# Fewer slots for two experts, norms by scaled transposes, and a modulation group weighed by VectorE

## The chip, the cores and the metric

The kernel runs on one core of one Trainium2 chip. The core has a matrix engine (TensorE, PE in the rows), three engines for element-wise work (VectorE or DVE, ScalarE or ACT, GpSimd or POOL) and SyncE (SP), whose instructions here do little but start transfers. Sixteen DMA engines move data between memory and the core. The metric is the device time of one execution in microseconds; before the change it is 1521.48 us, the median of three runs.

## What is computed

The reference is a two-layer network over 256 latent tokens and 256 context tokens of width 1024. Each layer has a token mixer (attention, retention and pooling between one input and one output projection) and then a channel mixer, each between two norms. The channel mixer of the first layer is a dense gated block for both streams. That of the second layer sends each of the 256 latent tokens to two of eight experts. Cut to what the change touches:

```python
for i in range(2):
    sh1, sc1, g1, sh2, sc2, g2 = split(silu(c) @ w_mod[i] + b_mod[i], 6)   # and the same from c_ctx
    hx = rms_norm(x, norm_pre_mix[i]) * (1 + sc1) + sh1
    x = x + g1 * rms_norm(token_mixers(hx, hc, ...), norm_post_mix[i])
    hx = rms_norm(x, norm_pre_ffn[i]) * (1 + sc2) + sh2
    x = x + g2 * rms_norm(ffn(hx), norm_post_ffn[i])     # dense in layer 0, experts in layer 1

def swiglu(h, w1, w3, w2):                                # 1024 -> 2816 -> 1024
    return (silu(h @ w1) * (h @ w3)) @ w2

def moe_swiglu(h, router, w1, w3, w2):
    top_vals, top_idx = lax.top_k(h @ router, 2)          # two experts for each token
    gates = sum(one_hot(top_idx, 8) * softmax(top_vals)[..., None], axis=-2)
    return sum(gates[..., e:e+1] * swiglu(h, w1[e], w3[e], w2[e]) for e in range(8))
```

Everything is float32. With the reference's inputs the router gives the eight experts 15, 154, 50, 25, 52, 46, 80 and 90 tokens.

## The kernel before

One program runs through five stages: setup, the first layer's mixer, the dense block, the second layer's mixer, and the experts. The order of each engine's instructions is set when the program is built, by a scheduler that starts from the order of the text and what each instruction needs; a block of text can be held back behind another instruction (`behind`). Buffers come from pools by a tag; a new tile of a tag with all its buffers in use waits for the readers of the oldest one.

**Experts.** Each expert has a fixed number of slots (`SLOTS`), and only that many rows are computed for it. Position 0 is expert 0; positions 1 to 7 are the other experts by falling number of tokens, which VectorE works out from the router's result. `RUNS` says in which order the positions are computed: position 0 first, then 2, 4, a run with two positions side by side, 5, 3, 7. The two that share a run are position 1, which has 160 slots in two parts of 128 and 32, and position 6 with 64. If any expert has more tokens than slots, a loop behind the output goes through its weights again for the rest.

The weights of one expert are 33 blocks of 1 MB: 22 of w1 and w3 in turn (`up`), and 11 of w2 (`down`). SyncE loads them in that order (`wload`, L172) into a ring of 13 buffers; six more are lent once at the start of the stage. A load waits until the ring's next buffer has been read. For a part of 128 slots each matrix product is done in three passes (`mm3`, L235 to L237) on operands that VectorE and ScalarE split into a high and a low half (L161, L162). For fewer slots it is plain float32 with the features as the stationary operand, and several matmuls stand side by side in the array: with 64 slots two of 64 rows by 256 columns, with 32 slots four of 32 rows by 128 columns (L1339 in `up`; L1368 in `down`, with 512 and 256 columns). A matmul of the text in float32 shows as two records in the trace.

The rows of an expert's tokens come to the core in two ways. For position 0 matmuls with a selection matrix `P` pick them (L1281). For the others the kernel writes all rows scaled by their norm to a table in memory (`xrows`), works out the numbers of the rows (`index`, L1223), gathers them with an indirect DMA (`fetch`, tile `xr`), and transposes them (L1278, in `gather`). This is done for the next run while the matmuls of `up` of the current one go on. In `act` the products become activations: silu on ScalarE, a product on VectorE, transposes on TensorE (L1306), tiles `mg`. `scatter` writes the results to memory; the last run instead adds its own to the sum of the others (`add_up`, `adder`, `combine`).

**Norms.** `prenorm` makes the transposed and modulated features of a block of 256 tokens. It is called four times: for the context (m = 1) and the latents (m = 0) ahead of the dense block, and for both ahead of the second layer's mixer. The rows are in two tiles of 128x1024. VectorE works out the reciprocal norm of each row (L444, L150 to L157) and multiplies a 128x128 identity with it (`diag`, L544); sixteen matmuls with the rows stationary and the diagonal moving scale and transpose in one (L551). Then come scale and shift (L559 on VectorE, and the same on ScalarE) and the split into halves.

**Modulation.** The vectors `sh1` to `g2` are products of silu(c) with `w_mod`, in groups of eight blocks of 1 MB (`mod_group`). The first `split` blocks of a group are weighed on VectorE (L369 for the first, L367 for the others, two instructions of 128x1024 a block and stream) and their sums are folded on TensorE at the end; the other blocks are multiplied on TensorE (L373). The last groups are pulled in as filler, a block at a time, between the steps of the dense block and of the second mixer (`fill`); the one that the change touches is group 2 of layer 1, for the latents alone, with `split` = `SPL` = 4.

Of the kernel before, what the change touches and what calls it, by code (L numbers as in the profile page):

```python
# [10 lines left out]
F32 = mybir.dt.float32  # L11
# [3 lines left out]
OP = mybir.AluOpType  # L15
# [5 lines left out]
D = 1024  # L21
KB = 8
# [7 lines left out]

SLOTS = (64, 160, 128, 128, 64, 64, 64, 64)

RUNS = ((0,), (2,), (4,), (1, 6), (5,), (3,), (7,))
SCRATCH = 4096
RING2, RING3 = 3, 6
MA = 3
NFILL, SPL, FILLS = 2, 4, (1, 1)
SPIN0, SPIN1, SPIN2 = 15, 5, 2  # L40

C_ID, C_TRI, C_IOTA, C_I8, C_CAP, C_TOK, C_ROW, C_COS, C_SIN, C_END = \
# [3 lines left out]
def shape_constants():  # L46
# [5 lines left out]
    c[:, C_I8:C_I8 + 8] = np.arange(8)  # L52
    c[:, C_CAP:C_CAP + 8] = SLOTS
    p = np.arange(128)
# [42 lines left out]
class Net:  # L97
# [437 lines left out]
    def prenorm(self, l, which, m, hh, hl):  # L535


        nc = self.nc
        A, B = self.modc[l][which], self.modc[l][which + 1]
        x = self.res_t[2 * m:2 * m + 2]  # L540
        diag = self.s2([128, 2, 128], "diag")
        for n in range(2):
            r = self.rstd([[x[n]]], [self.junk()])
            nc.vector.tensor_scalar(diag[:, n], self.ident, r[:, 0:1], None, op0=OP.mult)  # L544
        c = slice(256 * m, 256 * m + 256)
        for k0 in range(0, KB, 2):
            p = self.mm() if k0 % 4 and (l == 0 or m) else self.at()
            for k in range(2):
                for n in range(2):
                    s = 256 * k + 128 * n  # L550
                    nc.tensor.matmul(p[:, s:s + 128], lhsT=x[n][:, (k0 + k) * 128:(k0 + k + 1) * 128], rhs=diag[:, n],  # L551
                                     start=True, stop=True)
            h = self.s2([128, 2, 256], "h")
            for k in range(2):
                a, b = A[:, m, k0 + k:k0 + k + 1], B[:, m, k0 + k:k0 + k + 1]
                if k0 % 4:
                    nc.scalar.activation(h[:, k], p[:, 256 * k:256 * k + 256], AF.Identity, scale=a, bias=b)
                else:
                    nc.vector.tensor_scalar(h[:, k], p[:, 256 * k:256 * k + 256], a, b, op0=OP.mult, op1=OP.add)  # L559
            self.split(hh[:, k0:k0 + 2, c], hl[:, k0:k0 + 2, c], h)  # L560
# [596 lines left out]
    def experts(self, pool):  # L1157
        nc, I = self.nc, self.I
# [29 lines left out]
        p = self.at()  # L1188
        for t in range(2):
            for s in range(t + 1):  # L1190
                nc.tensor.matmul(p[:, t * 8:t * 8 + 8], lhsT=tri if s == t else onesr, rhs=sel[:, s],
                                 start=s == 0, stop=s == t)
# [64 lines left out]
            return xr, few  # L1257

        def group(n):
            return pool.tile([128, 4, 8 * n], F32, name="few", tag=f"few{n}", bufs=1 + n // 64)  # L1260

        def gather(base, n, rk=None, w=None, got=None):

            xr, few = got or (None, None)
            if xr is None:
                P = places("P", base, n, rk, w, 1)
            if n < 128:
                few = few or group(n)
                xs = few[:, 0].rearrange("p (k s) -> p k s", s=n)
# [3 lines left out]
            for q in range(2):  # L1273
                p = self.at()
                for k in range(4):
# [4 lines left out]
                    for t in range(2):  # L1280
                        nc.tensor.matmul(p[:, k * 128:k * 128 + n], lhsT=res[t][:, d:d + 128], rhs=P[:, t, :n],  # L1281
                                         start=t == 0, stop=t == 1)
                xg = xs[:, 4 * q:4 * q + 4] if n < 128 else pool.tile([128, 4, 128], F32, name="xg", tag="xg", bufs=1)
                for k in range(4):
                    kk = 4 * q + k
                    a, b = A[:, 0, kk:kk + 1], B[:, 0, kk:kk + 1]
# [4 lines left out]
                s = slice(4 * q, 4 * q + 4)  # L1291
# [132 lines left out]
        def ready(pos, t):  # L1424


            ns = [min(128, SLOTS[pos] - b) for b in range(0, SLOTS[pos], 128)]
            t[pos] = ns, [], []
# [45 lines left out]
        def last_sums():  # L1474
            pos, = RUNS[-1]
            return adder(0, SLOTS[pos], lambda t: rankp[:, t, pos:pos + 1], lambda t: gatep[:, t, pos:pos + 1], True)

# [79 lines left out]
        for i, run in enumerate(RUNS):  # L1557
# [5 lines left out]
            for pos in run:  # L1563
                ns, xs, _ = cur[pos]
# [11 lines left out]
            for c, aTs in enumerate(zip(*ups)):  # L1576
# [3 lines left out]
                else:  # L1580
                    hold.close()
                    if i == 0:
                        cur[0][2].append(index(0, 0, SLOTS[0])[1:])
            finish(side)
# [175 lines left out]
```

## Time and profile before

| | us |
|---|---|
| median of three runs (lowest, highest) | 1521.48 (1519.68, 1522.76) |
| the profiled execution: device time | 1520.14 |
| the profiled execution: span of the trace | 1517.9 |

| engine | busy us | share of the span | instructions |
|---|---|---|---|
| PE, matmuls | 1452.5 | 96% | 9006 |
| PEld, weight loads of TensorE | 1053.9 | 69% | 9007 |
| DVE | 823.6 | 54% | 1551 |
| ACT | 616.4 | 41% | 983 |
| POOL | 62.5 | 4% | 93 |

The trace covers one execution; its span starts with the first and ends with the last instruction, 2.2 us less than the device time. The table's shares are means over the five stages. The seven runs of the experts take from 800 us to 1502 us of the span, and the dense block ends with its norms between 635 and 660 us. The mean granted clock of TensorE is 0.985 of full speed. 410.8 MB are moved in all.

### The profile page before, as it was taken

Reading aid. Unit: us, or ns where it says so; the run is one execution under the profiler, and the core shown is the slowest. Engines: PE = TensorE matmul, PEld = TensorE weight load, DVE = VectorE, ACT = ScalarE, POOL = GpSimd, SP = SyncE. Lnnn points to the kernel's source line nnn. Section 1 sums busy time; section 2 is a strip of 40 time slices with the busy share of each in tenths; the row PEclk is TensorE's granted clock in tenths of the full one; section 3 lists DMA queues with packets and bytes.
Section 4 is the critical chain, followed back from the end, with each engine's and each line's share of the span. In section 5 each row is a group of like instructions: output and inputs, shape, how many; then the busy total and the mean of one; then the engine's idle time right before and its main releaser. Section 6 shows DMA issues by size and latency. Waiting matters only on the chain.

```text
span 1517.9 us, 22725 instructions
## 1 busy us (share of the span) xinstructions
PE 1452.5 (96%) x9006; PEld 1053.9 (69%) x9007; DVE 823.6 (54%) x1551; ACT 616.4 (41%) x983; POOL 62.5 (4%) x93
## 2 busy tenths in 40 slices
PE   7999999999999999999998999999999998999996
PEld 5677667988878888788665477764666655477762
DVE  3496687774554545778763088622454341078612
ACT  4336654423222222456641177522343331177511
POOL 1010200000000001000000010000000001010000
PEclk9999999999999999999999999999999999999998
DMA  8773223344453525353379899999998899999994
GB/s 340 278 285 146 86 98 123 141 170 163 142 206 135 207 100 186 119 186 111 118 293 420 351 416 368 370 403 419 419 355 329 326 363 393 420 421 409 409 420 180
DMA packets 62995, 410.82 MB, mean 271 GB/s; under 512 B 9428, under 2 KB 10136, under 8 KB 15648
## 3 DMA queue, kind: packets, MB, share of 16 engines
q1 hardware_dynamic: 54864, 392.19, 66.1%
q0 software_dynamic: 5616, 16.29, 2.9%
q8 instruction: 73, 1.20, 0.3%
q10 hardware_dynamic: 2400, 0.79, 0.2%
q14 instruction: 42, 0.34, 0.1%
HBM read 402.27 MB, written 6.98 MB: 270 GB/s over the span
## 4 chain that ended last, share of the span: by engine, by line
PE 84%; DVE 6%; DMA 5%; ACT 3%; issue 2%; ACTq 0%; POOL 0%; DVEq 0%; POOLq 0%
PE mm L1339 12%; PE mm L236 11%; PE mm L235 11%; PE mm L237 11%; PE mm L1368 7%; PE at L235 7%; PE at L236 7%; PE at L237 6%; PE md L373 1%; PE at L747 1%; DVE whl L162 1%; DMA more<-yrows 1%; DMA xr<-xrows,src 1%; PE at L724 1%; DMA few<-xrows,src 1%
## 5 line engine op out<-in xcount | busy, mean ns | idle before, releaser
L162 DVE TENSOR_TENSOR whl<-w,whl 128x1024 fp32r<-128x1024 f32 x310 | 374.5, 1223 | 267.6 <-ACT whl L161 259.2
L161 ACT ACTIVATE whl<-w 128x1024 fp32r<-128x1024 f32 x310 | 323.7, 1058 | 294.0 <-PE at L237 174.1
L1339 PE MATMUL mm<-w,few 128*64 128x256 f32 (+2 forms) x2528 | 225.8, 347 | 0.0
L1339 PEld LDWEIGHTS mm<-w,few 128*64 128x64 f32 (+1 forms) x2528 | 147.6, 133 | 68.6 <-issue 17.7
L1368 PE MATMUL mm<-w,few 128*64 128x512 f32 (+1 forms) x616 | 111.2, 536 | 0.0
L235 PE MATMUL mm<-hh,whl 128*128 128x512 f32 (+1 forms) x256 | 95.7, 374 | 1.2 <-ACT hh L161 1.2
L236 PE MATMUL mm<-hl,whl 128*128 128x512 f32 (+1 forms) x256 | 95.9, 375 | 0.0
L237 PE MATMUL mm<-hh,whl 128*128 128x512 f32 (+1 forms) x256 | 95.5, 373 | 0.0
L1368 PEld LDWEIGHTS mm<-w,few 128*64 128x64 f32 (+1 forms) x616 | 35.0, 129 | 70.6 <-issue 68.3
L237 PE MATMUL mm<-whl,hl 128*128 128x256 f32 (+1 forms) x240 | 80.9, 342 | 0.0
L236 PE MATMUL mm<-whl,hh 128*128 128x256 f32 (+1 forms) x224 | 75.3, 338 | 1.8 <-DVE whl L162 1.8
L1303 DVE TENSOR_TENSOR mg<-mg,mm 128x256 f32<-128x256 f32 (+2 forms) x36 | 13.6, 378 | 114.2 <-ACT mg L1302 114.2
L235 PE MATMUL mm<-whl,hh 128*128 128x256 f32 (+1 forms) x224 | 74.8, 338 | 0.0
L236 PE MATMUL at<-hl,whl 128*128 128x512 f32 (+1 forms) x192 | 71.3, 371 | 0.0
L237 PE MATMUL at<-hh,whl 128*128 128x512 f32 (+1 forms) x192 | 71.3, 371 | 0.0
L235 PE MATMUL at<-hh,whl 128*128 128x512 f32 (+1 forms) x192 | 71.2, 371 | 0.0
L367 DVE SCALAR_TENSOR_TENSOR wsum<-w,sc,wsum 128x1024 f32<-128x1024 f32 x48 | 59.7, 1281 | 20.8 <-DMA w<-in_w_mod_dram 20.8
L1302 ACT ACTIVATE mg<-mm 128x256 f32<-128x256 f32 (+3 forms) x54 | 22.8, 422 | 117.7 <-PE mm L1339 113.1
L235 PE MATMUL mm<-whl,xh 128*128 128x512 f32 (+1 forms) x144 | 57.9, 402 | 7.5 <-ACT whl L161 7.5
L236 PE MATMUL mm<-whl,xh 128*128 128x512 f32 (+1 forms) x144 | 57.2, 397 | 2.8 <-DVE whl L162 2.8
L235 PEld LDWEIGHTS mm<-hh,whl 128*128 128x128 f32 x256 | 48.2, 188 | 11.3 <-issue 2.1
L237 PE MATMUL mm<-whl,xl 128*128 128x512 f32 (+1 forms) x144 | 55.6, 386 | 0.0
(492 smaller groups left out, 2604.1 us busy)
## 6 DMA issues: line engine op xcount, KB each, us to landing
w<-in_moe_w_dram SPq DMA_DIRECT2D x258, 1024.0 KB, 11.5
w<-in_w_mod_dram SPq DMA_DIRECT2D x48, 1024.0 KB, 6.0
w<-in_ffn_w_dram SPq DMA_DIRECT2D x33, 1024.0 KB, 4.9
w<-in_w_in_dram SPq DMA_DIRECT2D x16, 1024.0 KB, 4.9
w<-in_w_out_dram SPq DMA_DIRECT2D x8, 1024.0 KB, 5.5
wa<-in_moe_w_dram SPq DMA_DIRECT2D x3, 1024.0 KB, 9.7
gate<-gscr POOLq DMA_DIRECT2D x5, 512.0 KB, 4.8
band<-in_band_dram SPq DMA_DIRECT2D x4, 512.0 KB, 7.8
```

The lines of the kernel that those rows point to most:

```text
L161: self.nc.scalar.activation(hi, x, AF.Copy)
L162: self.nc.vector.tensor_sub(lo, x, hi.bitcast(F32))
L235: mm(out, lhsT=a[0], rhs=b[0], start=start, stop=False)
L236: mm(out, lhsT=a[0], rhs=b[1], start=False, stop=False)
L237: mm(out, lhsT=a[1], rhs=b[0], start=False, stop=stop)
L367: nc.vector.scalar_tensor_tensor(x, y, c, x, op0=OP.mult, op1=OP.add)
L373: nc.tensor.matmul(p[32 * j:32 * j + 32], lhsT=self.sc[:, k], rhs=w[:, 0, j * 512:(j + 1) * 512], start=k == split, stop=k == KB - 1 and n ...
L724: nc.tensor.matmul(sp[:, :n], lhsT=qT[:, h, t * 128:t * 128 + 128], rhs=kT[:, kv, j, c0:], start=j == 0, stop=j == 1)
L747: nc.tensor.matmul(op[64 * i:64 * i + 64, side * 256:side * 256 + 256], lhsT=vt[:, b + 2 * side, kv * 64:kv * 64 + 64], rhs=src[:, b], sta ...
L1302: nc.scalar.activation(s1[:r, :c], h1[:r, :c], AF.Silu)
L1339: nc.tensor.matmul(h[i][m * j:m * j + m, :c], lhsT=x[0][:, k], rhs=t[:, k - k0, j * c:j * c + c], start=k == 0, stop=k == KB - 1, tile_pos ...
L1368: nc.tensor.matmul(y[0][m * q:m * q + m, :c], lhsT=x[0][:, b], rhs=w[:, j, c * q:c * q + c], start=f + j == 0, stop=f + j == FB - 1, tile_ ...
```

## The change

Four things change.

1. Position 0 and position 7, the one with the fewest tokens, get 32 slots instead of 64. Position 7 takes the place beside position 1, and position 6 goes into the last run.
2. `prenorm` no longer makes a diagonal. VectorE scales the rows themselves into a new tile `xs` (four instructions of 128x512 a call), and TensorE transposes them against the identity, in the same sixteen steps.
3. `SPL` goes from 4 to 8 (`KB`): all eight blocks of the last modulation group are weighed by VectorE.
4. The `few` tiles of 32 slots get two buffers like those of 64, and the tile `xg` of `gather` moves from a tag of its own with one buffer to the tag `mg`, which has two.

```diff
-SLOTS = (64, 160, 128, 128, 64, 64, 64, 64)
+SLOTS = (32, 160, 128, 128, 64, 64, 64, 32)
-RUNS = ((0,), (2,), (4,), (1, 6), (5,), (3,), (7,))
+RUNS = ((0,), (2,), (4,), (1, 7), (5,), (3,), (6,))
-NFILL, SPL, FILLS = 2, 4, (1, 1)
+NFILL, SPL, FILLS = 2, KB, (1, 1)
...
     def prenorm(self, l, which, m, hh, hl):
         x = self.res_t[2 * m:2 * m + 2]
-        diag = self.s2([128, 2, 128], "diag")
-        for n in range(2):
-            r = self.rstd([[x[n]]], [self.junk()])
-            nc.vector.tensor_scalar(diag[:, n], self.ident, r[:, 0:1], None, op0=OP.mult)
+        r = [self.rstd([[x[n]]], [self.junk()]) for n in range(2)]
+        xs = [self.s4([128, D], "xs") for _ in range(2)]
+        for half in range(2):
+            for n in range(2):
+                c = slice(512 * half, 512 * half + 512)
+                nc.vector.tensor_scalar(xs[n][:, c], x[n][:, c], r[n][:, 0:1], None, op0=OP.mult)
...
-                    nc.tensor.matmul(p[:, s:s + 128], lhsT=x[n][:, (k0 + k) * 128:(k0 + k + 1) * 128], rhs=diag[:, n],
-                                     start=True, stop=True)
+                    nc.tensor.transpose(p[:, s:s + 128], xs[n][:, (k0 + k) * 128:(k0 + k + 1) * 128], self.ident)
...
-            return pool.tile([128, 4, 8 * n], F32, name="few", tag=f"few{n}", bufs=1 + n // 64)
+            return pool.tile([128, 4, 8 * n], F32, name="few", tag=f"few{n}", bufs=2)
...
-                xg = xs[:, 4 * q:4 * q + 4] if n < 128 else pool.tile([128, 4, 128], F32, name="xg", tag="xg", bufs=1)
+                xg = xs[:, 4 * q:4 * q + 4] if n < 128 else pool.tile([128, 4, 128], F32, name="xg", tag="mg", bufs=2)
```

Three places show what the change does to the order of an engine's instructions. After the change every line behind `prenorm` has a number one higher.

TensorE in the first expert, from the last matmul that picks its rows (L1281) to the transposes of the second expert's gathered rows (tile `xr`). Here `few` is the features, `w` a block of weights, `facts` and `P` give the row numbers of a gather, and L1306 transposes activations. Before:

```order
L1281 MATMUL at<-P,res_2027 128x64
L1281 MATMUL at<-P,res_2028 128x64
L1339 MATMUL mm<-w,few 64x256 x32
L1223 MATMUL at<-facts,P 128x4 x2
L1339 MATMUL mm<-w,few 64x256 x11
L1306 MATMUL at<-cst,mg 128x128 x2
L1339 MATMUL mm<-w,few 64x256 x21
L1223 MATMUL at<-facts,P 128x4 x2
L1339 MATMUL mm<-w,few 64x256 x8
L1306 MATMUL at<-cst,mg 128x128 x2
L1339 MATMUL mm<-w,few 64x256 x24
L1278 MATMUL at<-cst,xr 128x128 x8
```

The same stretch of TensorE after the change:

```order
L1282 MATMUL at<-P,res_2027 128x32
L1282 MATMUL at<-P,res_2028 128x32
L1340 MATMUL mm<-w,few 32x128 x92
L1224 MATMUL at<-facts,P 128x4 x2
L1340 MATMUL mm<-w,few 32x128
L1307 MATMUL at<-cst,mg 128x128
L1340 MATMUL mm<-w,few 32x128 x35
L1224 MATMUL at<-facts,P 128x4 x2
L1340 MATMUL mm<-w,few 32x128 x16
L1307 MATMUL at<-cst,mg 128x128
L1340 MATMUL mm<-w,few 32x128 x48
L1279 MATMUL at<-cst,xr 128x128 x8
```

Between the rows of the first expert and those of the second stand 96 matmuls of 64x256 before and 192 of 32x128 after, which is twelve of the 22 blocks in both; the first numbers for the gathers stand behind 92 of the 192 instead of 32 of the 96.

VectorE at the end of the dense block, from the last weighings of the modulation group in the feed to the first residual (`acc`, and `pn`, its norm). Before:

```order
L367 SCALAR_TENSOR_TENSOR wsum<-w,sc,wsum 128x1024 x2
L1116 TENSOR_TENSOR a<-g,at 128x512
L162 TENSOR_TENSOR whl<-w,whl 128x1024
L162 TENSOR_TENSOR al<-a,ah 128x512
L162 TENSOR_TENSOR whl<-w,whl 128x1024
L1116 TENSOR_TENSOR a<-g,at 128x512
L162 TENSOR_TENSOR whl<-w,whl 128x1024
L162 TENSOR_TENSOR al<-a,ah 128x512
L1144 TENSOR_TENSOR acc_2535<-acc_2535,mm 128x512
L1144 TENSOR_TENSOR acc_2535<-acc_2535,at 128x512
L573 TENSOR_TENSOR pn<-acc_2535,gate 128x512 x2
```

The same place on VectorE after the change, from the weighings that follow those:

```order
L367 SCALAR_TENSOR_TENSOR wsum<-w,sc,wsum 128x1024 x2
L1117 TENSOR_TENSOR a<-g,at 128x512
L162 TENSOR_TENSOR whl<-w,whl 128x1024
L162 TENSOR_TENSOR al<-a,ah 128x512
L367 SCALAR_TENSOR_TENSOR wsum<-w,sc,wsum 128x1024 x2
L1145 TENSOR_TENSOR acc_2535<-acc_2535,mm 128x512
L1145 TENSOR_TENSOR acc_2535<-acc_2535,at 128x512
L574 TENSOR_TENSOR pn<-acc_2535,gate 128x512 x2
L444 SCALAR_TENSOR_TENSOR ms<-ss 128x1
L150 TENSOR_SCALAR rstd<-ms 128x1
L367 SCALAR_TENSOR_TENSOR wsum<-w,sc,wsum 128x1024
L151 TENSOR_TENSOR rsq_t<-rstd 128x1
```

Six of the eight new weighings stand among the block's last splits and activations (four of them in the rows above), and two stand one by one between the small steps of the first residual's norm.

VectorE at the dense block's start, in the second call of `prenorm` (m = 0), around the first weighings (L369) of a filler group. Before, in the second norm of the call:

```order
L150 TENSOR_SCALAR rstd<-ms 128x1
L369 TENSOR_SCALAR wsum<-w,sc 128x1024
L151 TENSOR_TENSOR rsq_t<-rstd 128x1
L444 SCALAR_TENSOR_TENSOR ms<-ss 128x1
L369 TENSOR_SCALAR wsum<-w,sc 128x1024
L152 SCALAR_TENSOR_TENSOR rsq_t<-rsq_t,ms 128x1
L150 TENSOR_SCALAR rstd<-ms 128x1
L369 TENSOR_SCALAR wsum<-w,sc 128x1024
```

The same weighings on VectorE after the change:

```order
L546 TENSOR_SCALAR xs<-res_2028,rstd 128x512 x2
L369 TENSOR_SCALAR wsum<-w,sc 128x1024
L560 TENSOR_SCALAR h<-at,modc_115,modc_116 128x256 x2
L369 TENSOR_SCALAR wsum<-w,sc 128x1024
L162 TENSOR_TENSOR hl<-h,hh 128x2x256 x2
L560 TENSOR_SCALAR h<-at,modc_115,modc_116 128x256 x2
L369 TENSOR_SCALAR wsum<-w,sc 128x1024
L162 TENSOR_TENSOR hl<-h,hh 128x2x256 x2
L369 TENSOR_SCALAR wsum<-w,sc 128x1024
```

They stood between the small steps that make the norms, ahead of the diagonals; now they stand behind the scaled rows, among the steps that take the transposed features out.

## Rows read from the trace of the kernel before

**Rows 1.** The page: DMA busy tenths and GB/s, 40 slices of the span.

```profile
DMA  8773223344453525353379899999998899999994
GB/s 340 278 285 146 86 98 123 141 170 163 142 206 135 207 100 186 119 186 111 118 293 420 351 416 368 370 403 419 419 355 329 326 363 393 420 421 409 409 420 180
```

**Rows 2.** Windows by run: length, busy PE, PEld, DVE, ACT, POOL; clock, DMA, GB/s.

```profile
800.40:872.50 72.10, 68.53 (x532) 39.61 (x530) 14.74 (x80) 11.78 (x26) 1.77 (x2) 0.98 0.95 384
872.50:975.00 102.50, 99.66 (x454) 78.94 (x454) 87.30 (x88) 76.51 (x84) 4.07 (x2) 0.98 0.99 389
975.00:1045.40 70.40, 66.96 (x520) 38.43 (x519) 10.03 (x39) 9.77 (x27) 3.75 (x4) 0.98 1.00 399
1045.40:1259.00 213.60, 208.78 (x1825) 135.13 (x1825) 93.28 (x101) 81.80 (x109) 4.96 (x3) 0.99 0.94 363
1259.00:1329.60 70.60, 64.82 (x497) 36.04 (x493) 5.95 (x18) 7.72 (x19) 3.81 (x4) 0.95 1.01 411
1329.60:1432.50 102.90, 99.52 (x456) 78.90 (x454) 86.84 (x86) 76.37 (x84) 4.69 (x3) 0.98 1.01 416
1432.50:1502.00 69.50, 66.08 (x498) 36.21 (x497) 5.58 (x10) 5.16 (x14) 2.45 (x3) 0.98 0.89 363
```

**Rows 3.** Waits of SyncE's load queue, 800 to 1500: total us, times, longest us.

```profile
SPq L172 <- PE mm L1339: 206.2, 97, 12.7
...
SPq L172 <- PE mm L1368: 83.3, 46, 4.6
```

**Rows 4.** Timeline of TensorE, first expert: start, us, instruction, records, idle before.

```profile
803.99 7.13 PE L1339 MATMUL mm<-w,few 128*64 128x256 f32 x64
...
830.63 1.09 PE L1278 MATMUL at<-cst,xr 128*128 128x128 f32 x8 [2.86 <-DMA xr<-xrows,src]
831.65 3.63 PE L1339 MATMUL mm<-w,few 128*64 128x256 f32 x16
...
853.38 19.10 PE L1368 MATMUL mm<-w,few 128*64 128x512 f32 x88
```

**Rows 5.** Timeline of TensorE, the pair (32 slots beside 128, later both in w2).

```profile
1079.31 1.08 PE L1339 MATMUL mm<-w,few 128*32 128x128 f32 x32
1080.32 0.50 PE L235 MATMUL at<-whl,xh 128*128 128x512 f32 x1
...
1239.68 2.94 PE L1368 MATMUL mm<-w,few 128*64 128x512 f32 x24
```

**Rows 6.** Window at the end of the last run, columns as in Rows 2.

```profile
1492.00:1496.00 4.00, 4.00 (x22) 1.36 (x20) 0.00 (x0) 0.00 (x0) 0.00 (x0) 1.00 0.39 158
```

**Rows 7.** Timeline of TensorE, the norm's matmuls at the dense block's start.

```profile
260.00 1.05 PE L551 MATMUL at<-diag,res 128*128 128x128 f32 x8
260.89 1.06 PE L551 MATMUL mm<-diag,res 128*128 128x128 f32 x8
```

**Rows 8.** Timeline of TensorE, transposes of 128x128 in another norm.

```profile
777.84 1.04 PE L1022 MATMUL at<-cst,res 128*128 128x128 f32 x8
778.63 0.48 PE L236 MATMUL mm<-whl,hl 128*128 128x512 f32 x1
```

**Rows 9.** VectorE by line: count, ns shortest/median/longest, first and last start.

```profile
L544 DVE TENSOR_SCALAR diag<-cst,rstd x8: 277/286/290, 255.8 to 651.3; 128x128 f32<-128x128 f32 x8
...
L369 DVE TENSOR_SCALAR wsum<-w,sc x8: 741/749/754, 268.2 to 525.2; 128x1024 f32<-128x1024 f32 x8
...
L367 DVE SCALAR_TENSOR_TENSOR wsum<-w,sc,wsum x48: 1276/1280/1286, 298.3 to 601.0; 128x1024 f32<-128x1024 f32 x48
```

**Rows 10.** Timeline of TensorE, a block of a modulation group.

```profile
89.58 1.92 PE L373 MATMUL md<-w,sc 128*32 128x512 f32 x16
```

**Rows 11.** Window at the dense block's end, columns as in Rows 2.

```profile
635.00:660.00 25.00, 24.28 (x181) 17.87 (x180) 23.85 (x92) 14.27 (x33) 2.57 (x5) 1.00 0.72 257
```

**Rows 12.** Waits of TensorE, 235 to 300 us: total us, times, longest us.

```profile
PE mm L235 <- ACT hh L161: 1.2, 1, 1.2
PE at L551 <- DVE diag L544: 0.6, 1, 0.6
```

## The prediction

> **What bounds the kernel now.** I read the page's slices first [rows 1]. The DMA digits are 2 to 5 in most of the first half and 8 or 9 from slice 20 on, where the experts' weights stream in; 420 GB/s is the most that any slice shows, and I take it as full rate: a 1 MB block each 2.5 us. An expert is 33 blocks (22 for w1 and w3, 11 for w2), so 82.5 us of stream if nothing holds it.
>
> Next the same counters cut by expert [rows 2]. TensorE is busy for 92 to 98% of each of the seven runs. The rate tells who waits for whom: 411 and 416 GB/s in the fifth and sixth run, but 384 in the first, 389 in the second and only 363 in the pair, the run of 213.6 us. In those the stream is held. By whom, the load queue's own waits say [rows 3]: 206.2 us for the matmuls of L1339 and 83.3 us for those of L1368, which are the readers that free the 13 ring buffers. At the very end [rows 6] the stream stops 1.5 us into the slice 1492 to 1496 (158 of 420 GB/s), and TensorE goes on to 1502, with the last block's 1.7 us as the only part that had to follow: 6.8 us of slack. So the chain of TensorE's work through the seven runs ends last, and the stream is close behind it. A gain on TensorE counts only as far as the stream can follow. It has this in hand: length times (1 - rate/420) is 6.2, 7.6, 3.5 and 29.0 us for the first four runs and 2.5 for the next two, 49 us together.
>
> **First expert in 32 slots.** Its matmuls hold 64 rows by 256 columns now, two side by side; then 32 by 128, four side by side. The price of the new form stands in the trace, because the expert of 160 slots has a part of 32: 32 records, one block, from 1079.31 to the next instruction at 1080.32, 1.01 us [rows 5]. The old form takes 7.13 us for 64 records [rows 4], 1.77 for a block's 16. For w2 the old form takes 19.10 us for 88 records [rows 4], 1.74 a block; the mixed row of 24 records in 2.94 us [rows 5] is one such block and one of the 32 slots, which leaves 1.20.
> The gain isn't 33 blocks of this. The order puts the transposes of the second expert's gathered rows (xr) after 12 of the 22 blocks, before and after alike (96 matmuls at 8 a block, 192 at 16). They run at 830.63 after a wait for that DMA [rows 4], which a chain of VectorE's tables and a write to memory sets and TensorE doesn't. After the change TensorE gets there some 10 us earlier and waits longer; nothing is won up to 830.6. From there: transposes 1.0, ten blocks at 1.01, one more us because the first block after a wait runs at half clock (831.65: 16 records in 3.63 us), 1.5 for transposes and the last activation, eleven blocks at 1.20: 830.6 + 1.0 + 10.1 + 1.0 + 1.5 + 13.2 = 857.4, where before it ended at 872.5 [rows 2]. I take 14.5 us of the 15.1. The stream allows that, near enough: it has 13.8 in hand by the end of the second run.
>
> **The pair.** The partner of the 160 slots drops from 64 to 32. 22 blocks at 1.77 - 1.01 are 16.7 us, 11 blocks at 1.74 - 1.20 are 5.9, six transposes fewer 0.6: 23.2 us. The dense three-pass matmuls of the 128 slots beside it don't change. Eight blocks then take some 21 us instead of 24, which asks the stream for 400 GB/s, just under full rate, and the ring starts this run emptier than before since the runs ahead are shorter. So waits for weights may appear: between 0 and 8 us (8 if the rate of the second run, 389, were all there is for the 66 blocks). I take 2.
>
> **The last run** now has 64 slots of the second least loaded expert instead of 64 of the least: same shapes, 69.5 us [rows 2], nothing. Second buffers for the 32-slot tiles and the shared buffer of xg are waits that no row shows; the nearest row is a 32-slot block, 1.01 us [rows 5]. I book 0, since each gather runs while TensorE has blocks of the run before it, and bound it by -1 (one block earlier) and +3 (one block late in each of the three gathers of 128).
>
> **Norms before the mixers.** Four calls. TensorE: sixteen fp32 matmuls are four rows of 8 records, 0.89 us from start to start [rows 7], 3.6 us; sixteen transposes are 16 records, 0.79 us per 8 [rows 8], 1.6 us. So 2.0 us a call less. VectorE: two scalings of 128x128 at 0.29 go, four of 128x512 come. By the 0.75 us of 128x1024 [rows 9] and the 0.29 of 128x128 these are 0.48 each: 1.4 us a call more. At the dense block's start TensorE waits 1.2 us for the first features and 0.6 for a diagonal [rows 12], and the order moves four weighings (0.75 each, 3 us) behind the second call's scaling, so its wait goes: -2 us. The two calls at the dense block's end lie where VectorE is busy 23.85 of 25 us [rows 11]; there 2 x 1.4 us more of VectorE is on the path, and the matmuls saved are hidden behind it: +2.8 less the 1 us that TensorE wins first.
>
> **Modulation group.** Four blocks leave TensorE: 32 records at 16 in 1.92 us [rows 10], 3.8 us. VectorE gets eight weighings at 1.28 us [rows 9], 10.2 us. The order puts six of them into VectorE's gaps in the last part of the dense block and two between the first residual's norm steps, 2.6 us on the path. What TensorE saves there was filler while VectorE finished the residuals. Cost +1.5, bounds -4 (all of TensorE's saving) and +10 (all of VectorE's).
>
> **Sum.** Front: -2 + 1.8 + 1.5, say +1. Experts: -14.5 - 23.2 + 2 = -35.7. The profiled execution took 1520.1 us (span 1517.9 and 2.2 around it); less 34.7 it is **1485**. The median of the runs shown is 1.3 us above the profiled one.
>
> **Rivals.** *The stream can't follow (1496).* If the DMA share [rows 2] is the true measure of idle time, not the rate, the stream has only 72.1 x 0.05 + 102.5 x 0.01 + 213.6 x 0.06 = 17.4 us in hand, with the end's 6.8 some 24: 1520 - 24 = 1496. For it: the share is 0.99 to 1.01 in four runs while the rate differs by 27 GB/s. Against it: at a share of 0.99 to 1.01 rates up to 420 stand in [rows 1], and with few loads in flight a packet's own time fills the share. Chance 0.12.
> *TensorE falls to half clock (1510).* The long wait ahead of 830 and the short bursts per block could leave TensorE at its 1.2 GHz level for the rest of the first expert. By the row at 831.65, 3.63 us instead of 1.77 [rows 4], its last 25 us become 50: 1485 + 25. Against it: that row is one block, the next 48 records take the full-clock time, and after the wait a backlog of landed blocks keeps TensorE busy. Chance 0.05. The Trainium skill, page "TensorE: Matmul & The Clock Gate", section "HAM oscillation — how this bites in real kernels", speaks against this change: bursts of thin matmuls shorter than the wait for their next data begin cold each time, and it advises padding them wider. By that rule every block of a 32-slot expert would be cold; in this trace the granted clock of every run is 0.95 or more [rows 2].
> *Slower: a count above 32 (1567 or more).* The place is the loop behind the output: one expert with more tokens than slots sends the program through its weights again, 33 blocks at 2.5 us, 82 us on top: 1485 + 82. It decides at the 33rd token of the first or the least loaded expert. Worked out from the reference's inputs the first has 15 and the least loaded 25, so it should not happen. Chance 0.02.
>
> **How the numbers follow.** Forecast 0.80, stream 0.12, clock 0.05, count 0.02, anything else 0.01. The forecast's own range goes from 1470 (front at -4, no waits, the stream's whole 49 us) to 1500 (front at +8, waits 8). To hold 8 in 10 I take 1470 to 1504, which adds the first rival. A difference of 0.2%, 3 us, is about what can be told from none here. Faster by more: 0.95; within: 0.02; slower: 0.03.
>
> **What would show it.** The first expert ends near 858 (+1) with a wait of about 12 us at xr; the pair takes 188 to 195 us at some 400 GB/s; the last three runs take 240 to 248 together as before (243.0); the residuals at the dense block's end start the second layer's projection no more than 3 us later. It would be wrong if the pair stayed above 205 us, if the first expert's blocks took over 1.3 us each, or if VectorE's weighings waited for their loads with the residuals queued behind them.

## The result and the profile after

The changed kernel takes 1478.79 us (median of four runs, 1477.56 to 1480.90) where the kernel before takes 1521.91 beside it: a ratio of 0.972, with a 95% interval of 0.9703 to 0.9737. The prediction was 1485, in a range of 1470 to 1504. The profiled execution took 1478.74 us with a span of 1476.4, 41.5 less than the span before.

The page of the changed kernel, first its span, then the DMA rows of its 40 slices, which answer to [rows 1]:

```profile
span 1476.4 us, 24170 instructions
...
DMA  9774222444435452623338999999999999999995
GB/s 343 271 286 173 94 100 72 143 171 171 171 124 205 171 194 106 237 80 116 113 141 361 420 413 409 420 415 414 418 408 419 409 418 420 420 409 419 421 419 205
```

The dips to 326 to 370 GB/s that the experts' stage had before are gone. From the 23rd slice on the rate stays at 408 to 421 GB/s up to the last slice. The same, cut by run as in [rows 2] (length; busy time of PE, PEld, DVE, ACT and POOL; granted clock, DMA share, GB/s):

```profile
808.60:863.20 54.60, 40.21 (x903) 32.14 (x902) 11.70 (x68) 10.44 (x26) 1.76 (x2) 0.87 1.01 415
863.20:964.00 100.80, 98.12 (x454) 77.91 (x454) 87.28 (x88) 76.30 (x84) 4.07 (x2) 1.00 1.01 416
964.00:1033.10 69.10, 66.91 (x520) 38.10 (x519) 9.87 (x39) 9.42 (x27) 3.69 (x4) 0.98 1.01 414
1033.10:1217.70 184.60, 178.79 (x2228) 130.44 (x2226) 92.63 (x101) 80.61 (x109) 1.90 (x2) 0.99 1.01 415
1217.70:1287.80 70.10, 65.32 (x499) 36.48 (x495) 5.74 (x18) 7.40 (x19) 3.91 (x4) 0.95 1.01 420
1287.80:1390.10 102.30, 99.49 (x454) 78.94 (x454) 86.86 (x86) 76.36 (x84) 2.46 (x3) 0.98 1.01 416
1390.10:1460.50 70.40, 66.11 (x498) 35.98 (x497) 5.57 (x10) 5.14 (x14) 2.45 (x3) 0.98 0.93 386
```

Counted from the first expert's first matmul in w1 (803.99 before, 808.64 after), the first run went from 68.5 to 54.6 us, the pair from 213.6 to 184.6, the other five together from 415.9 to 412.7. The stage starts 4.65 us later. So the sum is +4.65 - 13.9 - 29.0 - 3.2 = -41.5 us, all of the change in the span. (These are two single executions; what part of each term comes back in other executions is taken up below.)

Where the first expert's time goes is in TensorE's timeline, which answers to [rows 4] (start, length, instruction, records, the idle time before and what ended it):

```profile
808.64 5.23 PE L1340 MATMUL mm<-w,few 128*32 128x128 f32 x184
...
822.41 2.83 PE L1340 MATMUL mm<-w,few 128*32 128x128 f32 x96
835.31 1.97 PE L1279 MATMUL at<-cst,xr 128*128 128x128 f32 x8 [10.07 <-DMA xr<-xrows,src]
837.20 1.94 PE L1340 MATMUL mm<-w,few 128*32 128x128 f32 x32
838.91 1.84 PE L1340 MATMUL mm<-ws,few 128*32 128x128 f32 x32
...
841.17 2.83 PE L1340 MATMUL mm<-wa,few 128*32 128x128 f32 x96
...
847.43 0.43 PE L1340 MATMUL mm<-wb,few 128*32 128x128 f32 x8 [1.51 <-issue]
847.65 2.82 PE L1340 MATMUL mm<-w,few 128*32 128x128 f32 x64
850.39 0.33 PE L1307 MATMUL at<-cst,mg 128*128 128x128 f32 x1
850.65 1.94 PE L1340 MATMUL mm<-w,few 128*32 128x128 f32 x32
...
853.48 9.70 PE L1369 MATMUL mm<-w,few 128*32 128x256 f32 x176
```

TensorE is done with twelve blocks at 825.2 and then waits 10.07 us for the second expert's gathered rows. The gather is 4.68 us later than before, as is the whole stage. The first two blocks after the wait take almost twice the time of the three at 841.17 (0.94 each). The last two of the 22 take about 1.75 each at a granted clock of 1.00: `up` works in pieces of 512 columns, the last piece of 2816 has only 256, and its matmuls stand two side by side instead of four. Eleven blocks of w2 take 9.70 us, 0.88 each.

The end of the last run, where [rows 6] showed the stream stopping well ahead of TensorE. First the timeline of TensorE, then the chain that ended last:

```profile
1449.82 8.32 PE L1369 MATMUL mm<-w,few 128*64 128x512 f32 x38
1458.62 1.94 PE L1369 MATMUL mm<-w,few 128*64 128x512 f32 x8 [0.48 <-DMA w<-in_moe_w_dram]
```

```profile
1438.77 19.81 DMA w<-in_moe_w_dram
1458.58 0.04 issue
1458.62 1.96 PE mm L1369 x8
```

The last block lands at 1458.58 and its matmuls start at 1458.62. TensorE and the stream of weights now end together. Before, the last block landed at 1495.8, and TensorE ended its w2 at 1502.0: some 4.3 us of slack, if that block's matmuls take the 1.9 us that they take here. The slack is used up.

### The profile page after: what moved, and what is told of

It reads as the page before. It is cut to its first block, busy times and chain, and to the rows that moved or that the text cites. A ratio compares the mean times of both kernels' runs of the same rounds, so it can differ in the third digit from the quotient of the medians.

```text
span 1476.4 us, 24170 instructions
## 1 busy us (share of the span) xinstructions
PE 1388.4 (94%) x9716; PEld 1038.7 (70%) x9717; DVE 835.0 (57%) x1567; ACT 613.9 (42%) x983; POOL 57.2 (4%) x93
## 3 DMA queue, kind: packets, MB, share of 16 engines
q8 instruction: 78, 1.28, 0.4%
## 4 chain that ended last, share of the span: by engine, by line
PE 80%; DMA 8%; DVE 7%; ACT 3%; issue 1%; ACTq 0%; POOL 0%; DVEq 0%; POOLq 0%; SPq 0%
PE mm L235 11%; PE mm L236 11%; PE mm L237 11%; PE mm L1340 8%; PE at L235 7%; PE at L236 7%; PE at L237 7%; PE mm L1369 5%; DMA w<-in_moe_w_dram 4%; DMA xr<-xrows,src 2%; PE at L748 1%; PE at L725 1%; DVE whl L162 1%; PE at L736 1%; PE md L373 1%
## 5 line engine op out<-in xcount | busy, mean ns | idle before, releaser
L1340 PE MATMUL mm<-w,few 128*32 128x128 f32 (+2 forms) x3072 | 195.8, 316 | 1.0 <-issue 1.0
L1340 PEld LDWEIGHTS mm<-w,few 128*32 128x32 f32 (+1 forms) x3072 | 139.0, 123 | 50.9 <-issue 16.1
L1369 PE MATMUL mm<-w,few 128*32 128x256 f32 (+1 forms) x792 | 90.1, 452 | 0.5 <-DMA w<-in_moe_w_dram 0.5
L367 DVE SCALAR_TENSOR_TENSOR wsum<-w,sc,wsum 128x1024 f32<-128x1024 f32 x56 | 69.8, 1280 | 32.7 <-DMA w<-in_w_mod_dram 32.7
L1369 PEld LDWEIGHTS mm<-w,few 128*32 128x32 f32 (+1 forms) x792 | 34.6, 119 | 52.2 <-issue 39.2
L1303 ACT ACTIVATE mg<-mm 128x128 f32<-128x128 f32 (+3 forms) x54 | 21.7, 402 | 101.2 <-PE mm L1340 96.1
L1304 DVE TENSOR_TENSOR mg<-mg,mm 128x128 f32<-128x128 f32 (+2 forms) x36 | 12.2, 339 | 90.6 <-ACT mg L1303 90.5
## 6 DMA issues: line engine op xcount, KB each, us to landing
w<-in_moe_w_dram SPq DMA_DIRECT2D x258, 1024.0 KB, 18.4
```

What stands on the lines that cost most here:

```text
L367: nc.vector.scalar_tensor_tensor(x, y, c, x, op0=OP.mult, op1=OP.add)
L1303: nc.scalar.activation(s1[:r, :c], h1[:r, :c], AF.Silu)
L1340: nc.tensor.matmul(h[i][m * j:m * j + m, :c], lhsT=x[0][:, k], rhs=t[:, k - k0, j * c:j * c + c], start=k == 0, stop=k == KB - 1, tile_pos ...
L1369: nc.tensor.matmul(y[0][m * q:m * q + m, :c], lhsT=x[0][:, b], rhs=w[:, j, c * q:c * q + c], start=f + j == 0, stop=f + j == FB - 1, tile_ ...
```

## The experiments

All ratios are to the kernel before on the same chip, with 95% intervals.

**The parts by themselves.** The slots alone, with norms and modulation group as before:

```diff
-SLOTS = (64, 160, 128, 128, 64, 64, 64, 64)
+SLOTS = (32, 160, 128, 128, 64, 64, 64, 32)
-RUNS = ((0,), (2,), (4,), (1, 6), (5,), (3,), (7,))
+RUNS = ((0,), (2,), (4,), (1, 7), (5,), (3,), (6,))
...
-  name="few", tag=f"few{n}", bufs=1 + n // 64)
+  name="few", tag=f"few{n}", bufs=2)
...
-  name="xg", tag="xg", bufs=1)
+  name="xg", tag="mg", bufs=2)
```

> The slots alone: 32 slots for positions 0 and 7, the new runs and the tags of few and xg; norms and modulation group as before. In the trace after the change the first expert's matmuls start 4.65 us later than before (803.99 to 808.64) and the experts' stage is 46.1 us shorter. Theory: the 4.65 us come from the norms and the weighings alone, and the whole stage, its loads too, moves with its start, so this kernel takes 1478.8 - 4.65 = 1474 us. Rival: the stream of weights, which now runs at 415 to 420 GB/s all through the stage, sets the end whatever the front does, so the time stays at 1478.8.

Measured: 1479.97 us (1475.07 to 1486.63), 0.9717 (0.9702 to 0.9733). The slots carry the whole gain, and the front's 4.65 us do not come back when the norms and weighings are undone: the theory's 1474 lies below the interval (1476.6 to 1481.3). In this profiled execution the stage's first matmuls start at 808.34, though TensorE was only 1.16 us behind the kernel before when it began to pick rows, because those matmuls ran slow (granted clock 0.50 from 800 to 810). So the trace can't say what became of the earlier start; the last comparison below takes it up again.

The norms alone:

```diff
-        diag = self.s2([128, 2, 128], "diag")
...
+        xs = [self.s4([128, D], "xs") for _ in range(2)]
...
-                    nc.tensor.matmul(p[:, s:s + 128], lhsT=x[n][:, (k0 + k) * 128:(k0 + k + 1) * 128], rhs=diag[:, n],
-                                     start=True, stop=True)
+                    nc.tensor.transpose(p[:, s:s + 128], xs[n][:, (k0 + k) * 128:(k0 + k + 1) * 128], self.ident)
```

> The norms alone: scaled rows and transposes in place of the diagonals, all else as before. Theory: at all four calls VectorE's chain is what the mixers wait for, so the longer scaling costs and TensorE's shorter work is lost: +0.9 us at the dense block's start (as in the trace after), +1 to +3 at its end, 1521.9 + 2 to 4 = 1524 to 1526. Rival (TensorE's work counts, four calls by 2.0 us): 1514.

Measured: 1524.02 us beside 1521.98, 1.0012 (0.9999 to 1.0025). The rival's 1514 is excluded; a cost of some 2 us is likely but not certain. What the norms do to the front the trace tells more finely. TensorE comes to the first norm's first matmul [rows 7] without a wait, before and here, so nothing of the change shows up to there. From it to the first transposes of `kpk` in the second mixer (L676, L677 after the change) it is 413.7 us before and 418.6 here, 4.9 more.

The modulation group alone:

```diff
-NFILL, SPL, FILLS = 2, 4, (1, 1)
+NFILL, SPL, FILLS = 2, KB, (1, 1)
```

> The modulation group alone: all eight blocks weighed by VectorE. Theory: the two weighings between the first residual's norm steps lie on VectorE's path (2.6 us) and TensorE's saved matmuls were filler: +1 to +3 us, 1523 to 1525. Rival: TensorE's 3.8 us count, 1518.

Measured: 1520.29 us (1517.48 to 1529.00), 0.9995 (0.9977 to 1.0013): no difference that can be told. The rival's 1518 lies just outside the interval (1518.5 to 1524.0), the theory's 1523 to 1525 partly inside. In the trace the same stretch takes 416.2 us, 2.6 more than before. With both edits, in the changed kernel, it takes 418.6, so the two costs (4.9 and 2.6) do not add. The starts, in us of each span (timeline of TensorE):

| trace | first norm, L551 (L553) | `kpk`, L676 (L677) | between |
|---|---|---|---|
| before | 260.00 | 673.68 | 413.68 |
| norms alone | 259.65 | 678.22 | 418.57 |
| weighings alone | 259.99 | 676.23 | 416.24 |
| changed kernel | 259.78 | 678.36 | 418.58 |

For this stretch single traces can be compared: in the six traces with the old norms and weighings it takes 413.6 to 413.7 us, in the five with both edits 417.8 to 418.8.

What the two take from TensorE is shown by its waits between 630 and 665 us, where the changed kernel has

```profile
PE at L553 <- DVE xs L546: 8.0, 3, 4.5
PE mm L235 <- ACT hh L161: 1.6, 1, 1.6
PE md L380 <- DVE acc L1145: 0.6, 1, 0.6
```

(total us, times, longest us) and the kernel before one wait:

```profile
PE md L373 <- DVE acc L1144: 0.7, 1, 0.7
```

What TensorE was spared there turned into waiting, most of it for VectorE's scaled rows. The window that answers to [rows 11] says it again: PE is busy for 14.70 instead of 24.28 us, DVE for 24.02 instead of 23.85.

```profile
635.00:660.00 25.00, 14.70 (x97) 11.82 (x96) 24.02 (x85) 13.02 (x30) 3.18 (x6) 0.86 0.28 89
```

Next the two places of the slots. Position 0 alone, then the pair alone, each with the tags:

```diff
+SLOTS = (32, 160, 128, 128, 64, 64, 64, 64)
```

> Only the first expert in 32 slots (position 7 stays at 64 slots and in the last run, position 6 beside position 1; with the tags of few and xg). In the changed kernel the first run is 14.0 us shorter than before (68.5 to 54.5 us). Theory: TensorE's chain sets the end here, the stream has slack left, so the 14 us come out: 1521.5 - 14 = 1507 to 1508. Rival (a change of the first expert alone only makes the stream's later waits longer): 1512 or more.

```diff
+SLOTS = (64, 160, 128, 128, 64, 64, 64, 32)
+RUNS = ((0,), (2,), (4,), (1, 7), (5,), (3,), (6,))
```

> Only the pair: position 7 in 32 slots beside position 1, position 6 in the last run, position 0 stays at 64 slots (with the tags of few and xg). In the changed kernel this run is 29.0 us shorter than before (213.6 to 184.6 us), where the prediction had 21.2. Theory (the price of a 32-slot block of w2 was put too high and no wait for weights arose): 1521.5 - 29 = 1492 to 1493. Rival (part of the 29 us belongs to the other changes, by the earlier stream): 1498 to 1501.

Measured: 1508.63 us (1504.59 to 1511.86), 0.9915 (0.9899 to 0.9932), and 1488.99 (1485.02 to 1497.45), 0.9798 (0.9775 to 0.9821), beside 1521.72. That is 13.1 and 32.7 us; in the traces the first run takes 55.8 and the pair 184.4 us. Both theories hold within their intervals (1506.4 to 1511.4 and 1487.5 to 1494.5). Together 45.8 us, where the slots alone gave 42.0 and 42.4 in their two measurements. By the ratios the two parts together give 2.9% and the slots alone 2.8 and 2.7%, so a loss from having both isn't shown.

**Who ends last.** The changed kernel with the second expert's transposes moved behind 20 of the first expert's blocks:

```diff
                 yield
+            if pos == RUNS[1][0]:
+                yield
+                yield
             for n, got in due:
```

> The changed kernel, with the transposes of the second expert's gathered rows put behind 20 of the first expert's 22 blocks instead of behind 12. In the trace after the change TensorE waits 10.07 us for that gather, and at the end of the stage the last block lands at 1458.58 and its matmuls start at 1458.62. Theory (the stream is the bound now): the first expert ends some 7 us earlier, the later ones wait for weights or lose nothing, and the time stays within 1.5 us of 1478.8. Rival (TensorE's chain is the bound, as the prediction has it): the 7 us come out at the end, 1472.

Measured: 1479.95 us (1476.63 to 1482.32), 0.9724 (0.9708 to 0.9740). The theory's time; the rival's 1472 is excluded. In the trace the first run takes 47.3 us, 7.3 less than in the changed kernel, and by the time nothing of it arrives at the end: the last run takes 74.7 instead of 70.4 us, and there TensorE now waits for weights:

```profile
PE mm L1340 <- DMA w<-in_moe_w_dram: 4.9, 6, 1.7
PE mm L1369 <- DMA w<-in_moe_w_dram: 2.2, 4, 0.6
```

Then the stream was made shorter instead: 8 of the last expert's 11 loads of w2 are left out, and its matmuls read the third block again. After that both at once, beside the changed kernel again:

```diff
-                w = self.wload(w2(f), 2, D)
+                w = self.wload(w2(f), 2, D) if f < keep else w
...
+                                   6 if last else FB
```

> The changed kernel once more, beside the next three on the same chip: 1478.8 within 2 us. It is there so that differences of some microseconds to the others can be read at the same clock.

> The changed kernel without 8 of the last expert's 11 w2 loads: its matmuls use the third block again (so part of the weights is wrong there), 20 us of stream less, the same work on every engine. Theory (stream and TensorE end together in the changed kernel): TensorE's own chain still sets the end, so the gain is only its last waits, 0.5 to 2 us, 1477 to 1478.5. If the stream alone were the bound: -20 us, 1459.

> Both edits: the second expert's transposes behind 20 blocks of the first, and 8 of the last expert's w2 loads left out. Each alone should give at most 2 us, if TensorE's chain and the stream end together. Theory: with both out of the way the 7 us that the first expert ends earlier come out at the end, 1470 to 1473. Rival (something else than the stream took the late transposes' 7 us back, a wait on TensorE in the later runs): 1477 to 1480 as with either alone.

Measured: the changed kernel 1479.70 us (1477.13 to 1484.12), the short stream 1477.55 (1475.62 to 1480.61), both edits 1474.83 (1473.40 to 1475.66). So 20 us less of stream give 2 us, which isn't clear of noise (0.9698 to 0.9740 against 0.9717 to 0.9756 for the changed kernel), 7 us less of TensorE give none, and both together 5. The sign is as the theory says: two chains end together, and either edit alone runs into the other chain. In the changed kernel TensorE waits only 0.5 us for weights in the whole stage, so without the late transposes there was little for a shorter stream to give. The size is less than the 7 us expected and lies between theory and rival; in the run with both edits TensorE still waited 7.5 us for weights in all (5.1 in L1340, all of it in the last run, and 2.4 in L1369), and 20 us at the very end do not help blocks that are late earlier on.

**Where the front's 4.65 us went.** The slots alone again, beside the changed kernel of the last comparison:

> The slots alone once more (norms and modulation group as before). The first look gave 1480.0 and not 1474, with a profiled execution in which the matmuls that pick the first expert's rows ran at half clock. Theory 1 (that was the clock of those executions, the front's 4.65 us do count): at the clock at which the changed kernel takes 1478.8 this one takes 1474 to 1476. Theory 2 (the stream sets the end and takes the earlier start back): equal to the changed kernel within 1.5 us at the same clock.

Measured: 1478.76 us (1478.41 to 1481.69) against 1479.70, the same: theory 2's time. Yet its stage started at 802.31, that of the changed kernel at 806.39. The second to fourth runs take it back. First the changed kernel, then the slots alone:

```profile
861.10:962.00 100.90, 98.24 (x456) 77.92 (x458) 87.30 (x88) 76.38 (x84) 4.07 (x2) 1.00 1.01 416
962.00:1029.10 67.10, 65.24 (x519) 36.75 (x519) 9.86 (x39) 9.31 (x27) 3.68 (x4) 1.00 1.01 413
1029.10:1215.80 186.70, 180.40 (x2230) 131.51 (x2228) 92.60 (x101) 80.60 (x109) 1.90 (x2) 0.98 1.01 414
```

```profile
857.00:960.10 103.10, 99.74 (x457) 79.02 (x456) 87.29 (x88) 76.35 (x84) 4.07 (x2) 0.98 1.01 417
960.10:1031.30 71.20, 68.32 (x520) 39.48 (x519) 9.87 (x39) 9.39 (x27) 3.70 (x4) 0.95 1.01 412
1031.30:1218.80 187.50, 181.53 (x2230) 132.09 (x2228) 92.62 (x101) 80.65 (x109) 1.90 (x2) 0.97 1.00 403
```

The same records take 7.1 us longer in the second kernel, at a granted clock of 0.98, 0.95 and 0.97 instead of 1.00, 1.00 and 0.98. So in these two executions the 4 us were lost on TensorE's clock, with a stream that was held again in the pair (403 instead of 414 GB/s); that isn't theory 2's reason. The first traces of the two kernels say the same: these three runs take 359.6 us in the slots alone and 354.6 in the changed kernel. To see whether the first expert's wait has to do with it, the slots alone got the late transposes too (the edit shown above):

> The slots alone (norms and modulation group as before) with the second expert's transposes behind 20 of the first expert's blocks. The slots alone start the stage 4 to 6 us earlier and still took as long as the changed kernel; its profiled executions show more half-clock stretches from 840 us on. Theory 1 (the earlier start was given back in the first expert's wait of 11.7 us and the clock around it, where the stream was held too): without that wait the earlier start counts, 1473 to 1476. Theory 2 (the stream sets the end whatever TensorE does): 1478 to 1480.

Measured: 1472.75 us (1469.99 to 1476.65), 0.9681 (0.9665 to 0.9697). Theory 1 gave the time: without the wait the earlier start counts. This is the best kernel of the study, 0.4 to 0.6% below the changed one by the ratios (0.9681 against 0.9720 and 0.9737), some 6 to 9 us. It keeps only the slots and the tags from the change. The changed kernel with the same late transposes has 0.9724: once the wait is gone, the norms and the weighings cost some 6 us (3 to 10 by the intervals), and they make the front some 5 us longer. The granted clock over its second to fourth runs is 0.98, 0.98 and 0.99, between the two kernels above. Why it fell less than in the slots alone the runs don't settle: the wait goes and the stretches after it move, and which of them the clock follows wasn't tried apart.

In this kernel the stream sets the end outright. Its last run and TensorE's waits there:

```profile
1380.40:1455.00 74.60, 67.89 (x498) 35.31 (x497) 5.57 (x10) 5.03 (x14) 2.45 (x3) 0.98 0.92 382
```

```profile
PE mm L1339 <- DMA w<-in_moe_w_dram: 3.7, 4, 2.0
PE mm L1368 <- DMA w<-in_moe_w_dram: 2.2, 4, 0.6
```

The first nineteen blocks go to buffers that are free at the start. From the landing of the twentieth block to that of the last, its weights took 639.3 us (813.7 to 1453.0). In the changed kernel these are 638.9 us (819.7 to 1458.6), in the slots alone 646.0 (811.4 to 1457.4), and before 681.9 (813.9 to 1495.8). Some 639 us, or 2.62 a block, is thus what the 244 blocks take in two kernels whose twentieth blocks land 6 us apart. I take it as the length of a stream that nothing holds; that it can't be shorter isn't shown. Along the stream the change reads: twentieth block 5.8 us later, 43.0 us less to the last, 4.3 us of slack at the end used up, 41.5 us in all.

## Why the prediction was right, and where its steps were off

**What bounds the kernel.** Right. TensorE's chain through the runs was the bound, the stream was held, and a gain on TensorE counted as far as the stream could follow. How far that is was put at 49 us plus 6.8. By the landings the stream could come in 43 us faster, since a block takes 2.62 us and not 2.5: between these two landings the changed kernel moves 414 GB/s, of which the weights are 400 (244 blocks in 638.9 us), and gathers, scatters and tables the rest. The 6.8 counted from where the bulk of the transfers stops [rows 6]; the last packets of the last block took until 1495.8, which leaves 4.3. The change used up all of it. (Two small misreadings of [rows 1] change nothing: the digit at slice 20 is 7, and one slice shows 421 GB/s.) The load queue's waits, from which the prediction read who holds the stream, did not go when the stream was held no longer; the rows that answer to [rows 3] are

```profile
SPq L172 <- PE mm L1340: 129.3, 70, 9.3
...
SPq L172 <- PE mm L1369: 48.2, 33, 4.7
```

so they name the readers of the buffers and not what is lost. The rival with 24 us in hand (1496) fell: a DMA share of 0.99 to 1.01 says little about idle time, and the rate was the better measure, as the text against it had it. By [rows 2], a packet of 8 KB took about 0.333 us at a share of 0.99 and 389 GB/s and 0.318 at 1.01 and 416 (an estimate, as if all packets had that size): each took longer, and the share stayed.

**First expert.** Forecast 14.5 us and a wait of about 12 at xr; seen 13.9 and 10.07. The end was to be 858 and came at 863.2, almost all of it the late start. Within the run errors cancel. The price of a w2 block was 1.20 and is 0.88, 3.5 us less. The stretch from the gathered rows to w2 was put at 13.6 us and is 18.2 (835.31 to 853.48). Three things make up most of the 4.6. Transposes and two blocks after the wait ran at half clock, some 2.6 us, where one block was booked (the granted clock of this run is 0.87, where it was 0.98). The last two of the 22 blocks stand two side by side and not four, which costs 1.7 to 1.9 us; the price of 1.01 came from a row with four, and neither the prediction nor the description of the kernel tells the two apart. And TensorE stood still for 1.51 us ahead of 847.43, for no reason that the trace names. Blocks at 0.92 instead of 1.01 give a little back. So the clock rival did happen, for the transposes and two blocks and not for all the rest. The Trainium skill, page "TensorE: Matmul & The Clock Gate", section "HAM oscillation — how this bites in real kernels", has bursts of thin matmuls that are shorter than the wait for their next data start cold after each such wait. The trace agrees: the two blocks behind the wait of 10.07 us took 1.94 and 1.84 us, the three at 841.17 that follow without a wait 2.83 together. The prediction's reading, that by this rule every block of a 32-slot expert would be cold, left out that it is the wait that makes a burst cold.

**The pair.** Here the prediction was furthest off: 184.6 us, forecast 188 to 195, a gain of 29.0 instead of 21.2. (Its step from 24 to 21 us for eight blocks does not come from the rows: 213.6 us for 66 blocks are 25.9 for eight. The 400 GB/s hang on it; the pair shows 415.) Two terms failed, the price of w2 and the wait. TensorE's groups of instructions in this run say how much (matmuls of L1339 and L1368 and their count; busy us, mean ns of one; idle before), first of the kernel before, then of the changed one:

```profile
L1339 PE MATMUL mm<-w,few 128*32 128x128 f32 (+2 forms) x1088 | 69.5, 311 | 0.0
L1368 PE MATMUL mm<-w,few 128*32 128x256 f32 (+1 forms) x266 | 35.4, 460 | 0.0
```

```profile
L1340 PE MATMUL mm<-w,few 128*32 128x128 f32 x1408 | 51.1, 275 | 1.0 <-issue 1.0
L1369 PE MATMUL mm<-w,few 128*32 128x256 f32 (+1 forms) x354 | 23.5, 384 | 0.0
```

In w1 and w3 18.4 us went (forecast 16.7), in w2 11.9 (forecast 5.9). For w2 I had read the mixed row of 2.94 us a block [rows 5], subtracted the 1.74 of a 64-slot block among its like, and so booked on the 32-slot part all that the mixed row has above the two forms among their like, 0.32 us by the 0.88 of the first expert. Two parts of 32 slots next to each other take less:

```profile
1177.84 1.93 PE L1369 MATMUL mm<-w,few 128*32 128x256 f32 x32
```

That is 0.97 for each of the two, and 1.01 us less than the mixed row where 0.54 was booked. The other 2 us had been booked for waits for weights in the pair, and none arose: among TensorE's waits from 1033.1 to 1217.7 there is none for `in_moe_w_dram`. With 0.6 us of transposes these rows give 30.9 us; the run as a whole is 29.0 shorter.

**Last run, second buffers, xg.** The last three runs took 242.8 us where 240 to 248 were forecast. Among TensorE's waits in the stage none names one of these buffers; the tags weren't tried apart from the slots. The 3.2 us of the five other runs were booked at nothing, and hang on the clock of the execution: the second run takes 100.8 us at 1.00 in the changed kernel and 103.1 at 0.98 in the slots alone, where it took 102.5 at 0.98 before.

**Norms.** Forecast -2 us at the dense block's start. There VectorE's first product of the dense block (L1116) starts 28.3 us behind the first norm's first matmul before and 29.6 after (28.32 and 29.55): 1.2 us later. The step that failed is that the weighings, moved away from the small norm steps, would free VectorE for 3 us. The steps did get shorter: they are 0.2 us apart where a weighing between them made it 0.7, and from the first of them to the second residual it is 4.0 us instead of 6.8. But the `pn` products that they need have come behind the first call's features, so they start 2.3 us later (269.00 instead of 266.75). What is left, half a microsecond, goes on the longer scaling and on the weighings, which now stand between the steps that take the features out. Also, what the first call wins on TensorE (its first dense matmul starts at 263.02 instead of 264.91) is gone at the second, which waits for VectorE: 1.1, 1.2 and 0.9 us there, 0.6 before.

At the dense block's end +1.8 was forecast for the norms and +1.5 for the weighings, 3.3; seen were 3.7 (from 1.2 late to 4.9 late). That sum held, the split did not: the norms alone cost 3.7 there as well, the weighings alone 2.6, as long as the two that stand between the small steps of the first residual (1.28 each, priced in the prediction at 2.6 and booked at 1.5). The sign that the second layer's projection starts no more than 3 us later failed: the same stretch ends 4.9 us later.

**The sum.** Front +4.65 instead of +1, experts -46.1 instead of -35.7 (the other five runs, booked at nothing, gave 3.2). The two errors have opposite signs, so the sum missed by less than the experts' part alone: that much of the 1485 is luck. The front's error and most of the experts' came from prices taken at a shape or an order that the new code does not have.

## What to carry to other kernels

Price a new shape from a row where it stands next to its like, and if only a mixed row exists, keep both ends: the change of shapes costs something, and it goes away when the neighbours are alike. Before a gain on one engine is booked, work out how long the other chain is when nothing holds it; here that length (639 us of stream, not known ahead) is what the change ran into, and from there on only edits to both chains paid. Costs on one engine's chain need not add: the norms alone made the front 4.9 us longer, the weighings alone 2.6, and both together 4.9. To read a cost of a few microseconds from single traces, measure from a point just ahead of the first edit, as with the front here.

## What the runs showed of the hardware

Executions of one and the same kernel differ with the granted clock of TensorE. Of 23 of the kernel before, those with a mean of 0.985 to 0.986 took 1519.2 to 1522.8 us, those with 0.980 took 1525.0 and 1525.4, and one with 0.976 took 1532.2. I had read the clock as a loss of one block after a wait. It is larger: behind the wait of 10.07 us the transposes and two blocks ran at half clock, and in the second to fourth runs of the slots alone, at 0.98, 0.95 and 0.97, a start 4 us earlier was lost. Why the clock fell there more than in the changed kernel isn't shown. A second difference lies ahead of all edits: the first norm's matmuls started at 256.89 us in one execution of the changed kernel and at 259.78 in another. Comparisons of a few microseconds between two kernels here need several executions each, and a single trace can mislead: the profiled execution of the weighings alone took 1529.0 us, the median of its twelve 1520.29.
